# Projections as seven half products in a dense stage, both SSD scans run side by side with the plain rest of q and k

## The chip, the cores and the metric

The kernel runs on one core of a Trainium2 chip. Time is device microseconds of one execution. The engines are named as in the profile: PE is TensorE (matmul and transposes), PEld its weight load, DVE is VectorE, ACT is ScalarE, POOL is GpSimd, SP is SyncE, which issues all the DMAs here.

## The reference

One decoder layer over L = 1040 positions (16 meta tokens and 1024 real ones), width 1024, float32:

```python
h = rms_norm(x)                                   # (L, 1024)
z, xbc, dt, q, k, v = split(h @ W_in)             # 1024, 1024+2*256, 16, 1024, 1024, 1024 columns
# state-space half (SSD): 2 groups of 8 heads of 64, state 128, chunks of 128
xbc = silu(causal_dwconv4(xbc)); dt = softplus(dt + bias)
y[c] = (C B^T * decay) (x dt) + exp(cumsum) C prev;  prev = prev * chunk_decay + B^T (x dt decay)
y_ssd = rms_norm((y + D x) * silu(z))
# stick-breaking attention: 16 heads of 64
beta = sigmoid(q k^T / 8);  A[t,s] = beta[t,s] * prod_{s<j<t} (1 - beta[t,j]);  y_sb = A v
h += rms_norm([y_ssd ; rms_norm(y_sb)] @ W_out)
h += rms_norm((gelu(dwconv3(h W_g)) * (h W_u)) @ W_down)      # 2816 wide
```

## The kernel before

A float32 product is made of three fp32r matmuls: each operand is split into a high part (ACT casts it, `wh`, `whi`) and the rest (POOL subtracts it, `wl`, `wlo`), and hi·hi, hi·lo and lo·hi are added up in PSUM. Weights are split in tiles of 128x1024 by `load_w` (L155 on ACT, L156 on POOL).

The stages, in the order of the program:

- **Head.** x is loaded, normalised, transposed and split; the columns B0, C0 and dt are projected.
- **Projections.** `project_steps` (L169) makes one tile of 128 output columns at a time, over three ranges of tokens (400, 384 and 256 wide), with 24 matmuls for each: 8 blocks of 128 rows of W, three matmuls for each. The x, z, q, k and v columns are all made this way: `pj_X`, `pj_z`, `pj_q`, `pj_k`, `pj_v`. They are half steps of 12 matmuls, chained by `flow` and handed out by `run(fill, n)` between the small matmuls of the stages below, so that PE has work while the other engines prepare the next chunk or block.
- **Two scans**, one group after the other (155 to 402 us). For each of 9 chunks, `chunk_weights` makes the decay matrix (`sgh` on ACT, `sgl` on POOL at L627, matmul `sg`, `em` = exp on ACT, em times C·B at L641 on DVE) and two scaled copies of x (`xdt` at L644 on DVE, `yo` at L647 on POOL); `chunk_outputs` adds what the state gives (`yo` plus `yt` at L666 on DVE) and makes the next state (`xw` L670 and the sum L681 on DVE, `pv` L678 on POOL); `chunk_store` transposes, multiplies by silu(z) and sums the squares (L704 and L707 on POOL).
- **Attention** (404 to 897 us). For 8 pairs of heads p and 8 blocks of 128 queries i: `z` = q·k (L782); ACT takes both sigmoids, `kp` and `bt` (L783, L784); DVE runs a product scan over the keys, backwards, once for each head (`kp` and `hold`, L790); POOL multiplies `bt` by `kp`, once for each head (L792), and fills the edge `cb` (L793); PE transposes `bt` (`tw`, L804), ACT copies it (`th`), PE multiplies by v (`av`, L819). Block i has 144 + 128 i keys. z of a block stands three blocks ahead of its `tw` on PE; `kp` has two buffers, `bt` three. `split_q` splits q in each block on DVE (L758, L759). The fill between is q, k and v of the next pairs, and at the end the first steps of the output projection `mo`. v is transposed on PE (`vtp`).
- **Output projection, feed-forward, down projection**, to the end. The feed-forward and the down projection already use seven half products in place of eight (Strassen's scheme in Winograd's form: `fA`, `fX`, `fY`; `dnA`, `dnB`).

PE, DVE, ACT and POOL follow a written order in the feed-forward and the down projection; in the scans and the attention PE follows the order of the program and a scheduler orders the other engines.

## Time and profile before

| | |
|---|---|
| runs (us) | 1717.05, 1719.15, 1720.05; median 1719.15 |
| span of the profiled execution (us) | 1716.6, granted clock 0.999 |
| time of the profiled execution | not listed apart; the median is 2.55 us over its span |
| busy (us) | PE 1697.0, PEld 1495.9, DVE 1107.7, ACT 821.7, POOL 834.0 |
| scans 155 to 402 us, busy | PE 246.5, DVE 169.4, ACT 126.5, POOL 154.1 |
| attention 404 to 897 us, busy | PE 490.7, DVE 327.5, ACT 307.1, POOL 291.1 |
| DMA | 173.87 MB, 101 GB/s over the span |

A busy engine is one with an instruction in progress; an instruction that has started and is held up inside counts as busy. The duration of a matmul holds its fill and drain, so the pace of PE is read from one start to the next.

### The profile page before, as it was taken

The page shows a single profiled execution, that of the slowest core. Times are in us where ns is not written, and L with a number is a line of the kernel's source. Part 1 is how long each engine was busy: PE and PEld are TensorE (multiplying, and loading weights), DVE is VectorE, ACT ScalarE, POOL GpSimd, SP SyncE. Part 2 cuts the span into 40 slices and gives each one's busy share as a digit, 9 for nine tenths or more (in the row PEclk, how much of TensorE's full clock was granted, in tenths as well). Part 3 has the DMA queues.
Part 4 walks back from the last instruction along what each step waited for, and adds up shares of the span by engine and source line. Part 5 has one row for each costly group of instructions (what it writes and reads, how often), then busy time and mean ns, then how long its engine had stood idle before and what let it go on. Part 6 is the DMA issues. An engine that isn't in the chain of part 4 may idle for free.

```text
span 1716.6 us, 28052 instructions
## 1 busy us (share of the span) xinstructions
PE 1697.0 (99%) x11230; PEld 1495.9 (87%) x11230; DVE 1107.7 (65%) x1234; ACT 821.7 (48%) x1370; POOL 834.0 (49%) x641
## 2 busy tenths in 40 slices
PE   7999999999999999999999999999999999999998
PEld 6999889888989998998788788999988888888886
DVE  6752973875676686576640567676666566658777
ACT  5423563554665566567652445433333333344544
POOL 4323663686556575564552222587766777400001
PEclk9999999999999999999999999999999999999999
DMA  4132433231011011112223654233323323395335
GB/s 165 52 117 93 111 117 119 63 105 44 26 38 38 26 38 38 38 51 74 77 68 132 220 171 136 68 111 104 111 94 93 93 92 93 115 333 195 99 112 182
DMA packets 90674, 173.87 MB, mean 101 GB/s; under 512 B 10704, under 2 KB 35816, under 8 KB 90544
## 3 DMA queue, kind: packets, MB, share of 16 engines
q1 hardware_dynamic: 90544, 172.08, 31.8%
q8 instruction: 88, 1.44, 0.3%
q14 instruction: 42, 0.34, 0.1%
HBM read 122.32 MB, written 49.73 MB: 100 GB/s over the span
## 4 chain that ended last, share of the span: by engine, by line
PE 96%; DVE 1%; ACT 1%; DMA 1%; issue 0%; POOL 0%; SPq 0%; DVEq 0%; POOLq 0%; ACTq 0%
PE mo L976 10%; PE fX L1342 10%; PE dnA L1754 7%; PE fA L1342 7%; PE fY L1342 7%; PE pj_v L169 6%; PE pj_k L169 5%; PE pj_q L169 5%; PE pj_z L169 5%; PE dnB L1754 5%; PE pj_X L169 5%; PE av L819 4%; PE z L782 4%; PE tw L804 4%; PE pj_B L169 1%; PE yt L692 1%
## 5 line engine op out<-in xcount | busy, mean ns | idle before, releaser
L792 POOL TENSOR_TENSOR bt<-bt,kp 128x256 f32<-128x256 f32 (+7 forms) x128 | 212.1, 1677 | 184.2 <-DVE kp L790 140.6
L790 DVE TENSOR_TENSOR_SCAN kp<-kp,hold 128x272 f32<-128x272 f32 (+7 forms) x128 | 183.4, 1473 | 24.6 <-ACT kp L783 14.3
L1292 POOL TENSOR_TENSOR wlo<-wr,whi 128x1024 fp32r<-128x1024 f32 x43 | 99.3, 2318 | 40.5 <-ACT whi L1291 40.5
L1791 POOL TENSOR_TENSOR fms<-fms 128x1 f32<-128x1 f32 x8 | 2.5, 316 | 221.9 <-DMA ar<-fda 185.8
L783 ACT ACTIVATE kp<-z 128x288 f32<-128x288 f32 (+6 forms) x112 | 82.7, 739 | 50.7 <-PE z L782 25.8
L1291 ACT ACTIVATE whi<-wr 128x1024 fp32r<-128x1024 f32 x43 | 45.7, 1063 | 111.0 <-PE fX L1342 67.5
L169 PE MATMUL pj_v<-xs,wh_v 128*128 128x400 f32 (+2 forms) x384 | 95.0, 334 | 0.0
L169 PE MATMUL pj_k<-xs,wh_k 128*128 128x400 f32 (+2 forms) x384 | 94.6, 333 | 0.0
L1676 ACT ACTIVATE dh<-ar 128x512 fp32r<-128x512 f32 x77 | 48.6, 631 | 94.6 <-PE dnB L1754 44.7
L169 PE MATMUL pj_q<-xs,wh_q 128*128 128x386 f32 (+2 forms) x384 | 93.8, 331 | 0.0
L806 ACT ACTIVATE th<-tw 128x1024 f32<-128x1024 f32 (+2 forms) x96 | 75.5, 815 | 37.5 <-PE tw L804 37.2
L169 PE MATMUL pj_X<-xs,wh_X 128*128 128x400 f32 (+2 forms) x384 | 92.0, 326 | 0.0
L169 PE MATMUL pj_z<-xs,wh_z 128*128 128x386 f32 (+2 forms) x384 | 91.6, 326 | 0.0
L1414 DVE SCALAR_TENSOR_TENSOR ga<-gr,pp,ga 128x1024 f32<-128x1024 f32 x44 | 69.4, 1576 | 34.1 <-ACT ga L1407 33.4
L758 DVE CAST qh<-q 128x128 fp32r<-128x128 f32 x64 | 46.7, 731 | 68.9 <-PE z L782 68.5
L976 PE MATMUL mo<-woa,yh 128*128 128x512 f32 x256 | 85.5, 400 | 0.0
L1677 DVE TENSOR_TENSOR dl<-ar,dh 128x512 fp32r<-128x512 f32 x77 | 53.2, 691 | 47.2 <-ACT dh L1676 47.2
L784 ACT ACTIVATE bt<-z 128x288 f32<-128x288 f32 (+6 forms) x112 | 83.0, 741 | 0.0
L804 PE MATMUL tw<-ident,bt 128*128 128x128 f32 x576 | 75.7, 274 | 2.1 <-POOL cb L793 1.6
L819 PE MATMUL av<-th,v 128*64 128x128 f32 x1152 | 77.2, 278 | 0.0
L819 PEld LDWEIGHTS av<-th,v 128*64 128x64 f32 x1152 | 61.5, 136 | 13.8 <-issue 11.0
L804 PEld LDWEIGHTS tw<-ident,bt 128*128 128x128 f32 x576 | 65.4, 141 | 8.6 <-issue 3.1
(560 smaller groups left out, 5603.6 us busy)
## 6 DMA issues: line engine op xcount, KB each, us to landing
wr<-in_w_up SPq DMA_DIRECT2D x44, 512.0 KB
fds<-ga SPq DMA_DIRECT2D x44, 256.0 KB
b<-in_w_down SPq DMA_DIRECT2D x44, 256.0 KB
ar<-fds SPq DMA_DIRECT2D x44, 256.0 KB
fda<-ga SPq DMA_DIRECT2D x33, 256.0 KB
ar<-fda SPq DMA_DIRECT2D x33, 256.0 KB
yk<-yd SPq DMA_DIRECT2D x16, 512.0 KB
wor<-in_w_out SPq DMA_DIRECT2D x12, 512.0 KB
```

The costliest lines, as they stand in the source:

```text
L169: mm(acc[:ncol, :n - s], a[:, k, :ncol], xs[c0][:, b, k, s:n], start=(k == 0 and j == 0), stop=(k == KB - 1 and j == 2))
L783: nc.scalar.activation(kp[:, :, a:a + w], z[:, :, :w], AF.Sigmoid, scale=-QSCALE)
L784: nc.scalar.activation(bt[:, :, a:a + w], z[:, :, :w], AF.Sigmoid, scale=QSCALE)
L790: nc.vector.tensor_tensor_scan(kp[:, j][:, ::-1], kp[:, j][:, ::-1], hold[:, L - n:L][:, ::-1], 0.0, op0=ALU.mult, op1=ALU.max)
L792: nc.gpsimd.tensor_tensor(bt[:, j, 0:m], bt[:, j, 0:m], kp[:, j, 1:m + 1], op=ALU.mult)
L804: nc.tensor.transpose(tw[:, j, b, :], bt[:, j, c0:c0 + P], ident)
L806: copied[0] = nc.scalar.activation(th[:, :, :nb, :], tw[:, :, :nb, :], AF.Copy).ins
L819: mm(av[halves[j], :], v[:, kb, halves[j]], th[:, j, b, :], start=kb == 0, stop=kb == i)
L976: recent[0] = mm(acc, u[:, k, :], v[:, cs], start=(k == 0 and j == 0), stop=(k == 7 and j == 2))
L1292: nc.gpsimd.tensor_tensor(l, raw, h.bitcast(F32), op=ALU.subtract)
L1342: mm(acc[:, c, :nn], u[:, k, :], v[:, k, c0:c0 + nn], start=first and k == 0 and j == 0, stop=k == 3 and j == 2, skip_group_check=not first)
L1754: mm(banks[BANK[n], t], u[:, 0, c], v[:, 1, :], start=(n in (1, 2, 5) and p == 0 and i == 0), stop=(p == NPR - 1 and i == 2), skip_group_c ...
```

## The change

- **Dense stage.** x, z, the second B and C, and q and k of pairs 0 to 3 are made by 13 `Duo`s: two tiles of 128 columns each, over two halves of 520 tokens, as seven half products (`dA`, `dX`, `dY`) of 24 matmuls over 2 x 260 tokens in place of eight. The sums of token halves are made in the head (`t1` to `t4`), the sums of weights on POOL (`Duo.sums`), the sums of products on DVE. Convolution, silu and transposes of one duo are dealt out among the products of the next.
- **v** is made as tokens by channels, as seven half products of 128x512, so that the transposes of v go.
- Finished parts are stored in DRAM (`bcd`, `bnd`, `xsd`, `zd`, `qkd`, `vd`, `vcd`, `dtkd`) and loaded again where they are used. The first 16 rows of each block of v are copied from `vd` to `vcd`, DRAM to DRAM, ahead of the loads for the scans on SP's queue.
- **Both scans** run side by side, by chunk and then by group, 18 units. `xdt` and the sum `yo` + `yt` go from DVE to POOL; the squares are summed by one DVE reduction a chunk in place of additions on POOL.
- q and k of pairs 4 to 7 stay plain (`qk_fill`): 64 half steps of 12 matmuls over 260 columns, 4 ahead of the scans, 30 in them, 30 in the attention.
- **Attention**: q, k (already split) and v come from DRAM. The fill is 30 half steps of q and k, 9 short halo steps and 14 half steps of `mo`, spread evenly over the 64 blocks. The code of a block is otherwise the same (`L790` is L1106 now, L792 is L1108).

```diff
-CH = [(0, 400), (400, 384), (784, 256)]
+TH = L // 2
+CQ = TH // 2
+NQA = 4
+SCAN_FILL = 30
+OUT_FILL = 14
...
+    class Duo:
+        def sums(self):
+            r1, r2 = self.r
+            sub = nc.gpsimd.tensor_tensor
+            s24 = self.s24 = sa.tile([P, KB, P], F32, tag="s24", name=f"s24{self.nm}", bufs=1)
+            sub(r2[:, HI4], r2[:, HI4], r2[:, LO4], op=ALU.add)
+            sub(r2[:, LO4], r1[:, LO4], r2[:, LO4], op=ALU.subtract)
+            sub(s24[:, LO4], r2[:, HI4], r1[:, LO4], op=ALU.subtract)
+            sub(s24[:, HI4], r1[:, HI4], s24[:, LO4], op=ALU.subtract)
+        def product(self, n):
+            wn, xn, a, first = SPEC[n]
+            (hi, lo), (xh_, xl_) = self.w[wn], xo[xn]
...
+            for c in range(2):
+                for k in range(4):
+                    for j, (u, v) in enumerate(((hi, xh_), (hi, xl_), (lo, xh_))):
+                        mm(acc[:, c, :CQ], u[:, k, :], v[:, k, c * CQ:(c + 1) * CQ],
...
-            nc.vector.tensor_tensor(xdt[:nr], xsc, dt[:nr, c, hs].unsqueeze(2).to_broadcast([nr, 8, 64]),
+            nc.gpsimd.tensor_tensor(xdt[:nr], xsc, dt[:nr, c, hs].unsqueeze(2).to_broadcast([nr, 8, 64]),
...
-                nc.vector.tensor_tensor(yo[:nr], yo[:nr], yt[:nr], op=ALU.add)
+                nc.gpsimd.tensor_tensor(yo[:nr], yo[:nr], yt[:nr], op=ALU.add)
...
-            for b in range(0, 4, 2):
-                nc.gpsimd.tensor_tensor(sqk[:, b, ts], sqk[:, b, ts], sqk[:, b + 1, ts], op=ALU.add)
...
+            if g == 1:
+                nc.vector.tensor_reduce(out=sq[:, c0 + y0:c0 + nr],
+                                        in_=squares.pop(c)[:, :, ts].rearrange("p b t -> p t b"),
+                                        op=ALU.add, axis=mybir.AxisListType.X)
+        units = [(g, c) for c in range(NT + 1) for g in range(2)]
+        for n, (g, c) in enumerate(units):
+            nxt = chunk_weights(*units[n + 1]) if n + 1 < len(units) else None
+            scan_fill()
+            yo, zk, prev[g] = chunk_outputs(g, c, *cur, prev[g])
+            scan_fill()
+            chunk_store(g, c, cur[0], cur[1], yo, zk)
+            scan_fill()
+            cur = nxt
...
-    def split_q(p, i):
-        q = heads[p][0][:, NM + i * P:NM + (i + 1) * P]
...
-        nc.vector.tensor_copy(qh, q)
-        nc.vector.tensor_tensor(ql, q, qh.bitcast(F32), op=ALU.subtract)
...
+    for t in range(NT):
+        nc.sync.dma_start(out=vcd[NM * t:NM * t + NM], in_=vd[(t + 1) * P:(t + 1) * P + NM])
```

POOL in the scans, before: one chunk of one group in a steady stretch (`wl_z` belongs to the fill).

```order
L678 TENSOR_TENSOR pv_4_2277<-pv_3_2104,cdec 128x512
L647 TENSOR_TENSOR yo_5_2182<-xk_5_2153,dskip 128x512
L627 TENSOR_TENSOR sgl_6_2329<-tri,adl 128x1024
L704 TENSOR_TENSOR sqk_3_2148<-sqk_3_2148 128x128 x2
L707 TENSOR_TENSOR sq<-sqk_3_2148 128x128
L156 TENSOR_TENSOR wl_z_2570<-wr_z_2568,wh_z_2569 128x1024
```

POOL in the scans, now: the units of both groups in one chunk (`dtk` holds dt, its split parts and the decays).

```order
L940 TENSOR_TENSOR sgl_4_5148<-tri,dtk_4439 128x1024
L979 TENSOR_TENSOR yo_3_5007<-yo_3_5007,yt_3_5105 128x512
L991 TENSOR_TENSOR pv_4_5279<-pv_3_5112,dtk_4439 128x512
L957 TENSOR_TENSOR xdt_4_5172<-xk_4_5145,dtk_4439 128x512
L960 TENSOR_TENSOR yo_4_5174<-xk_4_5145,dskip 128x512
L940 TENSOR_TENSOR sgl_4_5240<-tri,dtk_4439 128x1024
L979 TENSOR_TENSOR yo_3_5099<-yo_3_5099,yt_3_5197 128x512
L991 TENSOR_TENSOR pv_4_5377<-pv_3_5204,dtk_4439 128x512
L957 TENSOR_TENSOR xdt_4_5264<-xk_4_5237,dtk_4439 128x512
L960 TENSOR_TENSOR yo_4_5266<-xk_4_5237,dskip 128x512
```

Two operations of 128x512 came to POOL for each unit, and the short additions of squares left it.

PE in the attention, before: from the transposes of block 4 of a pair to the products of block 5 with v, where z stands three blocks ahead.

```order
L804 MATMUL tw_4_0_4503<-ident,bt_4_4292 128x128 x8
L804 MATMUL tw_4_1_4514<-ident,bt_4_4292 128x128 x2
L169 MATMUL pj_q_400_4519<-xs_134,wh_q_4212 128x384 x2
L169 MATMUL pj_q_400_4519<-xs_134,wl_q_4213 128x384
L169 MATMUL pj_q_400_4519<-xs_134,wh_q_4212 128x384 x2
L169 MATMUL pj_q_400_4519<-xs_134,wl_q_4213 128x384
```

Now, at the same place of a pair:

```order
L1120 MATMUL tw_4_0_7479<-ident,bt_4_7314 128x128 x8
L1120 MATMUL tw_4_1_7490<-ident,bt_4_7314 128x128 x2
L1101 MATMUL z_7_0_7500<-qk_2_6685,qk_2_6681 128x348 x2
L1101 MATMUL z_7_0_7500<-qk_2_6685,qk_2_6683 128x348 x2
L1101 MATMUL z_7_0_7500<-qk_2_6687,qk_2_6681 128x348 x2
L1101 MATMUL z_7_1_7509<-qk_2_6685,qk_2_6681 128x348 x2
L1101 MATMUL z_7_1_7509<-qk_2_6685,qk_2_6683 128x348 x2
L1101 MATMUL z_7_1_7509<-qk_2_6687,qk_2_6681 128x348 x2
L1135 MATMUL av_4_7518<-th_4_0_7488,v_6847 64x128 x8
L1135 MATMUL av_4_7518<-th_4_1_7493,v_6847 64x128 x2
```

The fill behind the transposes is gone there; about one half step of 12 matmuls a block is left where two or more stood.

1028 lines of the change are left out of this document (636 added, 392 removed).

## Prediction, made before the changed kernel was run

> **What bounds the kernel now.** I read the page first, for the busy times and the chain that ended last:
>
> ```profile
> PE 1697.0 (99%) x11230; PEld 1495.9 (87%) x11230; DVE 1107.7 (65%) x1234; ACT 821.7 (48%) x1370; POOL 834.0 (49%) x641
> ...
> PE 96%; DVE 1%; ACT 1%; DMA 1%; issue 0%; POOL 0%; SPq 0%; DVEq 0%; POOLq 0%; ACTq 0%
> ```
>
> PE is idle for 1716.6 - 1697.0 = 19.6 us in all. So a matmul less is time won, as long as the others keep pace without it. The stretches by stage (columns: PE, PEld, DVE, ACT, POOL) tell how near they are, scans first, then attention:
>
> ```profile
> 155.00:402.00 247.00, 246.53 (x1620) 218.79 (x1621) 169.38 (x191) 126.47 (x274) 154.05 (x127) 1.00 0.35 100
> 404.00:897.00 493.00, 490.67 (x4068) 432.70 (x4067) 327.49 (x341) 307.13 (x513) 291.05 (x230) 1.00 0.15 45
> ```
>
> No engine but PE seems near its limit. But DVE and POOL hold each other up, which the sums hide. The timeline of both in the attention, DVE, then POOL:
>
> ```profile
> 616.56 3.51 DVE L790 TENSOR_TENSOR_SCAN kp<-kp,hold 128x784 f32<-128x784 f32 x2
> 620.44 1.06 DVE L758 CAST qh<-q 128x128 fp32r<-128x128 f32 x1 [0.37 <-PE z L782]
> 621.53 1.54 DVE L759 TENSOR_TENSOR ql<-q,qh 128x128 fp32r<-128x128 f32 x1
> 622.99 4.04 DVE L790 TENSOR_TENSOR_SCAN kp<-kp,hold 128x912 f32<-128x912 f32 x2
> ```
>
> ```profile
> 618.56 4.37 POOL L792 TENSOR_TENSOR bt<-bt,kp 128x768 f32<-128x768 f32 x2 [1.82 <-DVE kp L790]
> 622.87 0.30 POOL L793 TENSOR_TENSOR cb<-bt,kp 128x30 f32<-128x30 f32 x1
> ```
>
> ```profile
> L792 POOL TENSOR_TENSOR bt<-bt,kp x3: 412/1997/3840, 575.1 to 581.7; 128x1024 f32<-128x1024 f32 x2, 128x128 f32<-128x128 f32 x1
> ```
>
> Of two equal products of 128x1024, one lasted 3840 ns and the other 1997: the first began while the second scan was on DVE. At 618.56 the same: the second scan ended at 620.07, and the two products of 768 then took 2.86 us, 1.86 ns a column. And `ql` began at 621.53 and ended at 623.07, when POOL's products had ended (622.93). Each engine's instruction waits for the end of the other's. Where fill is thinnest, near 800 us, it goes on without a break:
>
> ```profile
> 801.69 3.47 DVE L790 TENSOR_TENSOR_SCAN kp<-kp,hold 128x784 f32<-128x784 f32 x2 [0.46 <-ACT kp L783]
> 806.62 2.47 DVE L905 SCALAR_TENSOR_TENSOR woa<-wor,pp,woa 128x1024 fp32r<-128x1024 f32 x1 [1.46 <-ACT woa L904]
> 809.02 1.26 DVE L962 TENSOR_TENSOR yl<-yk,yh 128x1024 fp32r<-128x1024 f32 x1
> ...
> 810.65 4.00 DVE L790 TENSOR_TENSOR_SCAN kp<-kp,hold 128x912 f32<-128x912 f32 x2
> 814.57 2.73 DVE L905 SCALAR_TENSOR_TENSOR woa<-wor,pp,woa 128x1024 fp32r<-128x1024 f32 x1
> ```
>
> ```profile
> 812.87 6.06 POOL L792 TENSOR_TENSOR bt<-bt,kp 128x896 f32<-128x896 f32 x2 [3.69 <-DVE kp L790]
> 818.89 1.22 POOL L793 TENSOR_TENSOR cb<-bt,kp 128x30 f32<-128x30 f32 x1
> ```
>
> From 810.65 to 818.93 scans, products and one split of `woa` stand end to end: 4.00 + 1.26 + 2 x 1.5 us. So for scans, products and their like the sum over both engines counts. In the attention before it was covered by 493 us of PE work. The change takes that cover away.
>
> **The change part by part.** Prices of PE, from the chain in order of time:
>
> ```profile
> 204.81 0.46 PE sg L634 x2
> 205.27 0.22 PE cb L638 x2
> 205.49 4.37 PE pj_X L169 x24
> 209.86 0.86 PE yf L662 x2
> 210.72 0.86 PE st L673 x2
> 211.58 4.17 PE pj_X L169 x24
> ```
>
> ```profile
> 389.31 2.87 PE pj_q L169 x24
> 392.18 0.44 PE vtp L428 x4
> 392.62 0.47 PE yt L692 x5
> ```
>
> ```profile
> 1110.44 2.88 PE fX L1342 x24
> ```
>
> ```profile
> 1503.86 26.75 PE dnA L1754 x118
> ```
>
> *Matmuls.* Counted in the order of the program, before: 28 groups of 24 at 4.37 (400 wide), 60 at 4.17 (384 or 386), 44 at 2.87 (256), and 72 transposes of v at 0.11: 122 + 250 + 126 + 8 = 506 us. Now: 127 groups of 24 over 260 columns at 2.88 (the feed-forward's 258 is the nearest row), 4 over 246 at 2.8, and 336 matmuls of 512 for v at 26.75 / 118 = 0.227, with 32 small ones: 366 + 11 + 76 + 3 = 456. dt loses 1. PE's work falls by **51 us**. If nothing else moved, the span would be 1716.6 - 51 = 1665.6.
>
> *Attention.* The columns of z over all blocks are 8 x 4736 = 37,888; PE's and POOL's own rows:
>
> ```profile
> 592.61 0.45 PE L782 MATMUL z<-kh,qh 64*128 64x400 f32 x2
> ...
> 593.36 1.97 PE L819 MATMUL av<-th,v 128*64 128x128 f32 x32
> ```
>
> ```profile
> 791.31 2.40 POOL L850 TENSOR_TENSOR sq<-sq,sqb 128x1024 f32<-128x1024 f32 x1
> ```
>
> z takes 0.75 us for 400 columns, 71 in all; 576 transposes at 0.11 take 63; 1152 `av` at 1.97 / 32 take 71. The fill is 30 x 12 matmuls at 0.12 = 43 and 14 x 12 at 0.227 = 38. PE: 286 us, where it was 491. DVE and POOL: the scans, 2 x 37,888 columns at 4.04 / 1824 = 2.2 ns, 168; the products, 73,728 columns at 1.9 ns (between 1.86 and 1.95), 140; 64 edges at 0.30, 19; six sums of squares at 2.40, 14; eight `woa` splits at 1.26 (`yl` has their size), 10. Together 351 us. The removed `split_q`, v's edges and the wl of v are already out of it. What is late next, then, is `tw`, which waits for `bt`; `z`, `av` and the fill stand behind it on PE. By blocks: block 7 needs 4.6 + 4.0 + 0.3 = 8.9 us of the pair, and PE has 1.95 + 1.76 + 1.97 + 1.3 = 7.0 for it; block 0 needs 1.4 against 2.3. The large blocks lose what the small can't give back. Term: 351 - 286 = **+65**. Bounds: 0, if the two engines were to run side by side (POOL alone has 173 and DVE 178), and +95, if each block also lost 0.5 us between hand-overs.
>
> *Scans.* Rows of the lines (ns: least, median, greatest):
>
> ```profile
> L627 POOL TENSOR_TENSOR sgl<-tri,adl x18: 393/1898/2893, 77.9 to 377.1; 128x1024 fp32r<-128x1024 f32 x16, 16x128 fp32r<-16x128 f32 x2
> L641 DVE TENSOR_TENSOR em<-em,cbm x18: 272/1638/2925, 157.5 to 385.1; 128x1024 f32<-128x1024 f32 x16, 16x128 f32<-16x128 f32 x2
> L644 DVE TENSOR_TENSOR xdt<-xk,dt x18: 674/764/2937, 127.4 to 382.4; 128x512 f32<-128x512 f32 x16, 16x512 f32<-16x512 f32 x2
> L647 POOL TENSOR_TENSOR yo<-xk,dskip x18: 1044/1204/1772, 127.5 to 384.1; 128x512 f32<-128x512 f32 x16, 16x512 f32<-16x512 f32 x2
> ```
>
> The gap between least and greatest is again the other engine. Undisturbed, a 128x512 takes 0.67 us on DVE and 1.04 on POOL, so moving `xdt` and `yo` + `yt` adds 2 x 0.37 to the sum of both, while the squares go from POOL. A unit now: `sgl` 1.90, four 128x512 on POOL 4.16, em times C·B 1.26, `xw` 0.67: 8.0 us; 16 units 128, the two short ones 6, four `wl` at 2.40 10: 144 us. PE: `sg` 0.92, `cb` 0.22, `yf` and `st` 1.72, 16 `yt` 1.5, so 4.4 a unit, 74 with the short ones, and fill 43: 117. The reduction of squares on DVE, eight times, reads one operand and lies beside PE's fill; I leave it at nothing, and 8 x 1.26 = 10 if it too must wait its turn. Term: **+27**; 0 if side by side, +45 if `sgl` and the rest stretch to their median as they did before.
>
> The Trainium skill (GPSIMD Engine Reference, section 4.1) calls POOL about twice as slow as DVE for operations with two inputs. By that the two moved would cost 1.34 each, and the scan term would be 10 us more; the rows say 1.55 times, and they stand.
>
> *Head, dense stage, boundaries.* Extra casts and differences in the head, waits of v's start for weights that are loaded into freed space, and the loads for the scans behind eight copies of `vcd` on SP show in no row. From below I take 5, from above the 19.6 us that PE idles now, twice. In the dense stage a pair of duos (x and z) asks POOL for about six splits of 128x1024 at 2.40 and eight sums of 128x512 at 1.04, and DVE for six taps and two scalings of 128x1040 at 1.26: 33 us beside 14 x 2.88 = 40 of PE, so it hides. Moves of `woa`, `qkd` stores and loads are hidden by 45 GB/s in the attention. Term: **+14**.
>
> *Sum:* 1716.6 - 51 + 65 + 27 + 14 = 1771.6, and the 2.55 us that the median lies over the span: **1774**. A difference under 0.2%, 3.4 us, could not be told from none.
>
> **Rivals.** *PE stays fed* (faster). Three blocks are under way at once, `bt` has three buffers, and a scan may wait less often than I sum up. Then the attention and the scans cost 10 together: 1716.6 - 51 + 10 + 14 + 2.5 = 1692. For it: before, PE lost only 493.0 - 490.7 = 2.3 us in the attention. Against: that stretch had 491 us of PE work. It decides where both terms fall below 35 together. The Trainium skill (SBUF — State Buffer, section "SBUF: two separate sides") bears on this: VectorE with two inputs from SBUF and GpSimd share a port pair, held for a whole instruction and never divided. The trace agrees wherever they meet (3840 against 1997 ns), but no row shows such a stage without PE's cover; by the rule the 351 us are a floor, and this rival falls.
>
> *The blocks' latency adds to it* (slower still). From the start of a block's scan (810.65) to the end of its products (818.93) pass 8.3 us, and PE stops at `tw` until then; `kp` has only two buffers, so ACT can't write the sigmoids of the block after next before the products of this one are done, and where ACT is late the two engines stand idle as well. Against: with 178 us of scans and splits beside 173 of products there is nearly always one waiting. At the upper bounds, 95 + 45 + 20: 1716.6 - 51 + 160 + 2.5 = 1828.
>
> *It comes out even.* Both terms at half (46) and a little at the boundaries: 1719.
>
> **How the numbers follow.** The sum as worked out, with terms between two thirds and the bounds: 0.68. PE stays fed: 0.15. Latency adds: 0.12. Even: 0.05. The likeliest gives 1774; its own range is 1735 to 1808. To hold 8 in 10 the range takes in the even case and part of the slow one: 1712 to 1812. Faster 0.15, same 0.05, slower 0.80.
>
> **What would show it.** Right: between the scans and the end of attention PE falls to about 80% busy, its idle time ends by `bt` or `cb` of POOL, and `bt` of 128x1024 often lasts over 3 us; the dense stage shows `dA`, `dX`, `dY` at 2.9 us for 24 without gaps; the scans take about 145 us, the attention about 350. Wrong: attention near 290 us with PE full, products at 2.0 us while scans run; or gaps of over 15 us at v's start or the scans' start.

## The result, and the profile after

The changed kernel takes 1831.2 us (median of 4 runs, 1828.8 to 1835.1), the one before 1719.6 (four runs now): ratio 1.066, 95% interval 1.064 to 1.068. The direction was forecast, the size was not: +112 us where the forecast had +54, outside its range of 1712 to 1812. The profiled execution has a span of 1831.3 us, 114.7 more than before.

First what the engines did. The page of the kernel after, busy time of each engine (part 1), and the granted clock in its 40 slices (part 2):

```profile
PE 1700.7 (93%) x11550; PEld 1465.1 (80%) x11550; DVE 1126.4 (62%) x1177; ACT 837.3 (46%) x1378; POOL 975.3 (53%) x687
...
PEclk9999999999799999998999999999999999999999
```

PE is busy 3.7 us longer than before, although it has less work, and idle for 1831.3 - 1700.7 = 130.6 us, where it was 19.6. Where, shows the busy time by stage: first before (head, scans, attention, rest), then after (head, dense stage, v, scans, attention, rest). The columns are the length, then busy us of PE, PEld, DVE, ACT and POOL, the granted clock, DMA share and GB/s.

```profile
0.00:154.50 154.50, 144.13 (x915) 137.31 (x915) 81.85 (x100) 60.04 (x106) 48.06 (x54) 1.00 0.34 110
154.50:401.00 246.50, 246.03 (x1619) 218.40 (x1618) 169.16 (x190) 126.42 (x273) 153.29 (x126) 1.00 0.35 100
401.00:917.70 516.70, 514.37 (x4255) 452.90 (x4253) 331.63 (x347) 315.70 (x524) 301.53 (x243) 1.00 0.15 45
917.70:1716.60 798.90, 792.49 (x4450) 687.26 (x4446) 525.02 (x597) 319.57 (x467) 331.08 (x220) 1.00 0.42 136
```
```profile
0.00:62.00 62.00, 42.87 (x305) 39.50 (x306) 47.16 (x60) 35.46 (x71) 26.16 (x41) 0.94 0.50 174
62.00:364.00 302.00, 287.07 (x2329) 283.47 (x2328) 152.46 (x146) 109.72 (x150) 184.77 (x107) 0.98 0.33 110
364.00:459.00 95.00, 89.53 (x455) 71.27 (x455) 41.60 (x40) 23.64 (x33) 19.96 (x8) 1.00 0.47 154
459.00:622.00 163.00, 136.85 (x893) 105.45 (x895) 108.68 (x126) 78.51 (x216) 122.25 (x87) 0.88 0.53 165
622.00:1031.00 409.00, 351.01 (x3122) 277.91 (x3122) 255.49 (x210) 269.44 (x442) 292.37 (x224) 0.96 0.28 89
1031.00:1831.30 800.30, 793.33 (x4456) 687.48 (x4452) 521.00 (x597) 320.55 (x467) 329.74 (x220) 1.00 0.42 136
```

Length less PE's busy time is PE's idle time: 58 us of the 131 are in the attention, 26 in the scans, 19 in the head, 15 in the dense stage. The clock column tells of a second loss: below 1.00, a busy microsecond does less work. Busy time times (1 - clock), summed over stretches of 4 us, is 2.7 us in the head, 5.8 in the dense stage, 17.1 in the scans and 14.6 in the attention: 40 us, an estimate from the rows, and about 1 before. What PE waits for, first in the attention, then in the scans, then in the head (us in total, times, longest):

```profile
PE z L1101 <- ACT th L1122: 35.3, 45, 4.3
PE tw L1120 <- ACT bt L1103: 12.6, 12, 4.3
PE z L1101 <- ACT bt L1103: 5.1, 8, 1.7
...
PE tw L1120 <- POOL bt L1108: 0.2, 1, 0.2
```
```profile
PE yt L1008 <- POOL yo L979: 21.2, 15, 2.9
PE sg L947 <- ACT sgh L938: 3.8, 1, 3.8
...
```
```profile
PE xtp L380 <- DVE xn L366: 14.9, 6, 8.4
...
```

In the attention, PE hardly ever waits for POOL. It waits for ACT: `z` and `tw` share two PSUM buffers, so `z` waits until ACT has copied `th` out of one, and `tw` until ACT has made the sigmoid `bt` from one. The scan and the product stretch as the prediction said (means 1.71 and 1.68 us), but PE's list has the product once, with 0.2 us, and the scan not at all:

```profile
L1106 DVE TENSOR_TENSOR_SCAN kp<-kp,hold 128x272 f32<-128x272 f32 (+7 forms) x128 | 212.6, 1706 | 106.1 <-ACT kp L1102 32.3
L1108 POOL TENSOR_TENSOR bt<-bt,kp 128x256 f32<-128x256 f32 (+7 forms) x128 | 212.5, 1679 | 103.8 <-DVE kp L1106 89.5
```

The clock, in stretches of 4 us at the start of the scans and in the middle of the attention (same columns):

```profile
472.00:476.00 4.00, 0.51 (x2) 0.30 (x2) 1.66 (x2) 2.49 (x9) 4.00 (x3) 1.00 0.10 33
476.00:480.00 4.00, 3.50 (x24) 2.43 (x24) 2.95 (x5) 1.30 (x3) 3.89 (x4) 0.52 0.33 79
480.00:484.00 4.00, 4.00 (x25) 2.88 (x25) 2.59 (x4) 0.48 (x1) 3.38 (x3) 0.50 0.75 154
484.00:488.00 4.00, 4.00 (x8) 1.58 (x7) 3.10 (x4) 3.15 (x11) 3.91 (x3) 0.50 0.32 37
488.00:492.00 4.00, 4.00 (x23) 2.76 (x22) 1.91 (x3) 0.00 (x0) 4.00 (x5) 0.50 0.64 198
...
848.00:852.00 4.00, 0.00 (x0) 0.00 (x0) 2.04 (x2) 2.22 (x4) 1.00 (x1) 0.95 0.71 218
852.00:856.00 4.00, 3.85 (x28) 3.39 (x30) 4.00 (x3) 3.16 (x6) 1.50 (x1) 0.50 1.03 421
856.00:860.00 4.00, 3.48 (x26) 2.91 (x24) 4.00 (x3) 1.52 (x3) 4.00 (x2) 0.70 0.61 244
```

After a stretch in which PE did next to nothing (0.51 and 0.00 of 4 us), it runs at half the clock, for 16 us and more the first time and some 6 the second; the matmuls show it too (one of `pj_k` over 260 columns lasts 0.42 us at 491.2 us and 0.28 at 497.4). The Trainium skill (TensorE: Matmul & The Clock Gate, section "HAM oscillation — how this bites in real kernels") gives the rule that PE should have no idle gaps over some 3.4 us; the trace agrees with it here, at 0.50 after gaps of 3.5 and 4.3 us. Shorter gaps were enough too: in the scans the clock was 0.57 from 510 to 514 and from 561 to 565 us, where the longest wait of PE just before was 2.3 us. The prediction did not count with any of it.

### The profile page after: what moved, and what is told of

Same layout as the page of the kernel before. It is cut to its first block, busy times and chain, and to the rows that moved or that the text cites. A ratio compares the mean times of both kernels' runs of the same rounds, so it can differ in the third digit from the quotient of the medians.

```text
span 1831.3 us, 29209 instructions
## 1 busy us (share of the span) xinstructions
PE 1700.7 (93%) x11550; PEld 1465.1 (80%) x11550; DVE 1126.4 (62%) x1177; ACT 837.3 (46%) x1378; POOL 975.3 (53%) x687
## 5 line engine op out<-in xcount | busy, mean ns | idle before, releaser
L1106 DVE TENSOR_TENSOR_SCAN kp<-kp,hold 128x272 f32<-128x272 f32 (+7 forms) x128 | 212.6, 1706 | 106.1 <-ACT kp L1102 32.3
L1108 POOL TENSOR_TENSOR bt<-bt,kp 128x256 f32<-128x256 f32 (+7 forms) x128 | 212.5, 1679 | 103.8 <-DVE kp L1106 89.5
L1101 PE MATMUL z<-qk,qk 64*128 64x328 f32 (+8 forms) x672 | 80.7, 356 | 41.3 <-ACT th L1122 35.3
L1101 PEld LDWEIGHTS z<-qk,qk 64*128 64x128 f32 x672 | 52.9, 192 | 64.4 <-ACT th L1122 49.4
L1120 PE MATMUL tw<-ident,bt 128*128 128x128 f32 x576 | 79.8, 281 | 15.5 <-ACT bt L1103 12.6
L1135 PE MATMUL av<-th,v 128*64 128x128 f32 x1152 | 83.0, 292 | 0.3 <-ACT th L1122 0.3
L1135 PEld LDWEIGHTS av<-th,v 128*64 128x64 f32 x1152 | 66.6, 145 | 14.5 <-issue 12.1
L1777 POOL TENSOR_TENSOR al<-wr,ah 128x512 fp32r<-128x512 f32 x20 | 28.7, 1433 | 76.9 <-ACT ah L1776 76.8
L2056 PE MATMUL dnA<-dl,dh 128*128 128x512 f32 x176 | 68.5, 389 | 0.0
L2056 PE MATMUL dnA<-dh 128*128 128x512 f32 x176 | 68.5, 389 | 0.0
L2056 PE MATMUL dnA<-dh,dl 128*128 128x512 f32 x176 | 68.5, 389 | 0.0
L2056 PE MATMUL dnB<-dh 128*128 128x512 f32 x132 | 51.3, 389 | 0.0
```

The lines of the kernel that those rows point to most:

```text
L1101: mm(z[:, j, :w], u[h, :], r[h, a:a + w], start=s_ == 0, stop=s_ == 2)
L1106: nc.vector.tensor_tensor_scan(kp[:, j][:, ::-1], kp[:, j][:, ::-1], hold[:, L - n:L][:, ::-1], 0.0, op0=ALU.mult, op1=ALU.max)
L1108: nc.gpsimd.tensor_tensor(bt[:, j, 0:m], bt[:, j, 0:m], kp[:, j, 1:m + 1], op=ALU.mult)
L1120: nc.tensor.transpose(tw[:, j, b, :], bt[:, j, c0:c0 + P], ident)
L1135: mm(av[halves[j], :], v[:, kb, halves[j]], th[:, j, b, :], start=kb == 0, stop=kb == i)
L2056: mm(banks[BANK[n], t], u[:, 0, c], v[:, 1, :], start=(n in (1, 2, 5) and p == 0 and i == 0), stop=(p == NPR - 1 and i == 2), skip_group_c ...
```

## The experiments

The prediction's reason is called the port theory below: VectorE and GpSimd, whose instructions were seen to wait for each other's end (3840 against 1997 ns in the prediction's row), set the length of both stages by the sum of their work. Its rival is the loop theory, in the attention also called the chain theory: one block or unit passes through TensorE, ScalarE, VectorE and GpSimd and back, in the order of each queue, and that chain sets the pace. Ratios are to the kernel before, measured along with each run; "against after" is the difference of the ratios times 1718 us. Stage times come from the profiled execution: length, idle time of PE and estimated slow clock, from the first `sg` to the first `z` (scans) and from there to the end of the last `av` (attention). Where its code was left as it is after, a profile showed the scans at 158 to 162 and the attention at 409 to 413, so a few us in a stage tell nothing.

| run | ratio, 95% interval | against after | scans: us, idle, slow | attention: us, idle, slow |
|---|---|---|---|---|
| after | 1.0659 (1.0639 to 1.0679) | | 162.3, 25.9, 17.1 | 409.8, 58.0, 14.6 |
| e1_bt_dve | 1.0566 (1.0547 to 1.0584) | -16 | | 395.7, 46.2, 14.8 |
| e2_scan_dve | 1.0629 (1.0606 to 1.0651) | -5 | 157.5, 22.0, 13.9 | |
| e3_dum_attn | 1.0906 (1.0889 to 1.0923) | +42 | | 455.7, 42.6, 9.3 |
| e4_dum_scan | 1.0680 (1.0663 to 1.0697) | +4 | 162.5, 10.1, 6.5 | |
| e6_fill_before_z | 1.0645 (1.0626 to 1.0665) | -2 | 158.3, 26.2, 13.0 | 408.5, 59.3, 15.1 |
| e8_scan_order | 1.0626 (1.0610 to 1.0642) | -6 | 151.6, 20.8, 10.9 | 411.0, 59.3, 16.1 |
| e9_all3 | 1.0424 (1.0402 to 1.0446) | -40 | 156.3, 20.0, 16.8 | 381.5, 36.8, 12.0 |
| e10_order_dve | 1.0642 (1.0626 to 1.0657) | -3 | 157.0, 26.1, 10.6 | |
| e13_dum_z | 1.0618 (1.0600 to 1.0635) | -7 | 160.5, 26.4, 15.5 | 406.5, 34.9, 6.7 |
| e14_zz3 | 1.0606 (1.0590 to 1.0621) | -9 | 158.4, 26.4, 13.0 | 403.3, 52.6, 16.0 |
| e15_bt4 | 1.0728 (1.0712 to 1.0744) | +12 | 157.7, 25.2, 12.8 | 433.0, 69.7, 17.4 |
| e22_deep_dve | 1.0627 (1.0612 to 1.0643) | -5 | 158.3, 26.3, 12.9 | 413.1, 53.4, 23.1 |
| e24_refill | 1.0642 (1.0621 to 1.0662) | -3 | 172.7, 17.8, 16.4 | 406.7, 63.2, 15.9 |
| e25_best | 1.0409 (1.0394 to 1.0425) | -43 | 157.9, 9.6, 9.5 | 380.6, 42.2, 13.9 |
| e26_sqb | 1.0658 (1.0642 to 1.0675) | 0 | 158.4, 26.3, 13.0 | 413.3, 56.2, 21.1 |
| e30_yo2x | 1.0745 (1.0726 to 1.0763) | +15 | 173.6, 34.6, 19.6 | |
| e31_scan_act | 1.0797 (1.0780 to 1.0814) | +24 | 184.4, 33.5, 20.7 | |
| e32_zz3_all | 1.0568 (1.0549 to 1.0587) | -16 | 151.9, 21.2, 10.9 | 403.6, 51.1, 21.3 |

**e1_bt_dve: the attention's products on VectorE.** The sum of both engines then has little of GpSimd left.

```diff
-            nc.gpsimd.tensor_tensor(bt[:, j, 0:m], bt[:, j, 0:m], kp[:, j, 1:m + 1], op=ALU.mult)
+            nc.vector.tensor_tensor(bt[:, j, 0:m], bt[:, j, 0:m], kp[:, j, 1:m + 1], op=ALU.mult)
...
-        nc.gpsimd.tensor_tensor(edges[p][:, :, i, 0:NM - 1], ...
+        nc.vector.tensor_tensor(edges[p][:, :, i, 0:NM - 1], ...
```

> The changed kernel with the products of bt and kp, and the edges, on DVE in place of POOL, in the attention only. Its attention lasts 414 us now (618 to 1032), of which PE idles 59.5 and loses about 14 to a lower granted clock. Port theory (DVE's scans and POOL's products exclude each other, 351 us in sum): DVE then has scans 168, products 73,728 columns at 1.04 ns 77, edges 10 and some 30 of other work, 285 us, less than PE's 326, so PE bounds again: attention about 345 us, kernel about 1763 us (-68), bt at about half of 1.9 ns a column with no instruction drawn out. Chain theory (a block's way through ACT, DVE, POOL and back to PE is too long for the three blocks in flight, whoever does the work): each block's way gets shorter by 0.9 us on average, a third of it counts: about -20 us, and PE still idles 45 us in the attention.

Measured -16, the stage 14 us shorter: what the chain theory said (-20), far from the port's -68. VectorE is busy 309.5 us there and GpSimd 38.0, held-up time included: 347 of 396 us, and PE still idles for 46. In this kernel the two engines' sum is not what holds the attention.

**e2_scan_dve: `xdt` and `yo` + `yt` back on VectorE**, where they were before the change.

```diff
-            nc.gpsimd.tensor_tensor(xdt[:nr], xsc, ...
+            nc.vector.tensor_tensor(xdt[:nr], xsc, ...
-                nc.gpsimd.tensor_tensor(yo[:nr], yo[:nr], yt[:nr], op=ALU.add)
+                nc.vector.tensor_tensor(yo[:nr], yo[:nr], yt[:nr], op=ALU.add)
```

> The changed kernel with xdt and the sum of yo and yt on DVE again, as before the change, in the scans only. The scans last 159 us now, PE idles 24.6 and loses about 17 to the clock. Port theory (sum of DVE's two-operand work and POOL's): 2 x 0.37 us less a unit, 12 us in 16 units: scans about 145 us, kernel about 1815 us (-16 with some of the clock). POOL theory (POOL alone is the bound, 7.2 us a unit): POOL loses 2.1 us a unit, PE bounds: scans about 122 us, kernel about 1793 us (-38). Neither (chain through the state): no change.

The scans take 157.5 us, within half a us of their spread, where the port theory had 145. The move of this work is not where the scans lost their time, and the sum of both engines alone does not set their length.

**e3_dum_attn and e4_dum_scan: TensorE work added**, whose results are overwritten: 18 matmuls of 128x128 ahead of `av` in each block, and 6 of 128x512 ahead of the `yt` products in each unit.

```diff
         av = psum_av(f"av{nm}")
+        for _ in range(18):
+            mm(av, identb, identb, start=True, stop=True)
```
```diff
             tp = psum_tp(f"yt{nm}")
+            for _ in range(6):
+                mm(tp.rearrange("p a b -> p (a b)"), xo["b22"][0][:, 0, 0:P], xo["b22"][0][:, 1, 0:512], start=True, stop=True)
```

> The changed kernel with 18 extra bf16 matmuls of 128x128 before each block's product with v, into the same PSUM tile, which the product then overwrites: about 1 us of PE work a block, 64 us in the attention, off the way from z to the transposes. Port theory: PE's own 326 plus 64 is 390, below the 414 that it lasts, so the kernel stays within 10 us of 1831, and PE's idle time falls by about 50. Clock theory (idle gaps of over 3 us bring half the clock for some us, 14 us lost in the attention): the granted clock there goes from 0.96 to about 1.00 and up to 14 us come back, so the kernel is equal or faster although it does more. If PE's work were the bound: +50 us or more.

> The changed kernel with 6 extra fp32r matmuls of 128x512 ahead of each unit's yt, into the PSUM tile that yt then overwrites: 1.4 us a unit, 24 us of PE work in the scans, at the place where PE waits for POOL's yo. Clock theory: the gaps before yt get too short to lower the clock, which goes from 0.88 to near 1.00 in the scans; 117 + 24 = 141 us of PE work fit in 159, so the scans get shorter by up to 17 us, kernel about 1817. If the clock costs nothing there (the engines that PE waits for set the pace): no change. If PE is the bound: +20 us.

In the attention 67 us of such work cost 42: at this place, between two hand-overs to ACT, work is on the path. In the scans 24 us of it cost some 4, inside the intervals, with the stage as long as before, and the idle time fell by 16 and the slow clock by 11: TensorE is not on the path of the scans at this place, and the half clock there fell into time that was waited anyway.

**e13_dum_z: the same kind of work where PE waits.** Nine of the small matmuls stand ahead of `z`.

```diff
+            av = None
+            if mix:
+                av = psum_av(f"avd{step}")
+                for _ in range(9):
+                    mm(av, identb, identb, start=True, stop=True)
             block = block_weights(p, i)
...
```

> In attention, 9 matmuls of 128x128 (bf16, overwritten later) per block just ahead of z, 62 blocks, about 32 us of TensorE work by what 18 of them cost ahead of av (67 us in 64 blocks, +43 us of time). Here they stand where TensorE waits for ScalarE's copy of tw, 35 us in 45 blocks. If the waits at this place are real slack: they cost 0 to 12 us (1831 to 1843), idle falls by 20 to 30, and the slow clock after gaps falls by 5 to 12 us. If work at this place delays the next hand-over to ScalarE by as much (TensorE's own part of the loop): +20 to +35.

The time does not rise; it falls by 7 us, with intervals that do not meet (1.0600 to 1.0635 against 1.0639 to 1.0679). The idle time fell by 23 us, the slow clock by 8. So in this place PE has slack, and filling it keeps the clock up. That it makes the kernel faster is less sure: of the 7 us the attention gave 3 (409.8 to 406.5), little outside the spread of 409 to 413.

**e6_fill_before_z: the plain products ahead of `z`.**

```diff
+            do(before)
             block = block_weights(p, i)
             next(block, None)
...
-            do(before)
             run(block)
```

> In attention, the plain output products of a block are issued ahead of its score products z instead of behind them, so that they stand between the transposes tw of an older block, whose PSUM buffers z takes over, and z. Nothing is added or left out. After spends 35.3 us of TensorE's idle time in attention in z waiting for ScalarE's copy th of tw, and 17.7 in z and tw behind the sigmoid bt. Theory 'no work between tw and z' (TensorE's order leaves nothing to do while ScalarE empties the shared buffers): most of the 35 goes and some comes back as waits of z's third chunk or of tw, -15 to -35 us against after (1796 to 1816), attention 375 to 395 instead of 410. Theory 'port' (VectorE and GpSimd together bound the stage): no change, within 5 us of 1831. Theory 'clock' (the slow stretches after gaps are a cost of their own): the slow-clock loss in attention, 14.6 us, falls along with the idle time.

The idle time only changed its name. PE's waits in this run from 622 to 1031 us (its attention is 614 to 1023):

```profile
PE z L1101 <- ACT th L1122: 19.1, 14, 4.3
PE tw L1120 <- ACT bt L1103: 11.1, 20, 1.4
PE tw L1120 <- POOL bt L1108: 9.5, 7, 2.8
```

Now `tw` waits for POOL's product, which the fill between `z` and `tw` had covered. The same fill can't stand in both places: that is the cover which the change has spent.

**e14_zz3, e15_bt4, e26_sqb: one resource of the attention more.** Three z/tw buffers, for which mo gets one accumulator and `av` shares a bank; four blocks under way; a buffer of its own for the squares.

```diff
-        return stage[0][1].tile([P, 2, 512], F32, tag="zz", name=name, bufs=2)
+        return stage[0][1].tile([P, 2, 512], F32, tag="zz", name=name, bufs=3)
...
```
```diff
-        btt = ap.tile([P, 2, L], F32, tag="bt", name=f"bt{nm}", bufs=3)
+        btt = ap.tile([P, 2, NM + (i % 4 + 5) * P], F32, tag=f"bt{i % 4}", name=f"bt{nm}", bufs=1)
-            if len(turn) > 2:
+            if len(turn) > 3:
```
```diff
-            sqt = ap.tile([P, 2, 4, P], F32, tag="th", name=f"sqb{p}", bufs=2)...
+            sqt = ap.tile([P, 2, 4, P], F32, tag="sqb", name=f"sqb{p}", bufs=1)...
```

> In attention, three double-bank PSUM buffers for z and tw instead of two; to make room, the plain products mo get one accumulator instead of two, and av shares one bank with the small turns (the sums of squares for r_ssd are taken in one go). Same work. After: attention 410 us, TensorE idle 58, of it 40 in z and 13 in tw, all behind ScalarE's copies and sigmoids of these buffers; with the fill moved ahead of z the idle time stayed (59) and only changed its name. Theory 'two buffers' (TensorE and ScalarE hand two buffers to and fro, and that hand-over sets the pace): a third lets TensorE run ahead, idle time falls by 25 to 45 us with some of the 14.6 us of slow clock: 1780 to 1805. Theory 'block latency' (TensorE waits for what ScalarE, VectorE and GpSimd need for one block, sigmoid, scan and product, and ScalarE is late because kp has two buffers): waits move from z to tw, within 8 us of 1831. Theory 'port': the same, no change.

> In attention, four blocks under way instead of three (four bt buffers, and tw of a block is issued one block later). Same work. Theory 'block latency': tw's waits for bt (13 us) go and, as ScalarE is no longer held up, part of z's: -15 to -40 us against 1831. Theory 'two buffers' (the hand-over of the z and tw buffers between TensorE and ScalarE sets the pace): within 8 us of 1831. Theory 'port' (VectorE and GpSimd bound the stage): within 5 us too.

> In attention, the squares of a head's outputs (sqb, 128x1024, once a head) get a buffer of their own instead of one of the two of th. Same work. After, ScalarE waits 12.0 us in the stage (3 times) with the copy th at the head of its queue, until GpSimd has added sqb into the sums, and everything behind it on ScalarE waits too. Theory 'head of ScalarE's queue' (TensorE's waits for th are in large part ScalarE waiting for GpSimd): -5 to -12 us. Theory 'port': no change (within 3 us). Theory 'closed loop with other waits ready to take over' (as the third buffer, the fourth block and the moved fill showed, -8, +13 and -2): within 4 us.

None of them is the cause alone: -9, +12 and 0 us. In e14_zz3 `z` waits 2.7 us for `th` instead of 35.3, but 14.1 for `bt`, and `avc` 10.3 in the bank that it now shares. In e15_bt4, which issues `tw` a block later, PE is idle for 69.7 us, and no theory had it slower. In its trace `tw` waits 8.7 us for POOL's `bt` (0.2 in after) and once 5.9 us for a load of `qk`, and `avc` 4.8 for DVE (0.9); whether these cost the 23 us is not shown.

**e22_deep_dve: all three of e1_bt_dve, e14_zz3 and e15_bt4**, the edges one block later. (Diffs as above.)

> All that loosens the attention together: three z/tw buffers, four blocks under way (the edges one block later), and bt*kp with its edges on VectorE. If the attention is bound by TensorE's own work once these are loosened: 340 to 360 us instead of 410, idle below 20, slow clock below 8: 1765 to 1785. If idle stays above 35 (as with bt*kp on VectorE and the fill moved, 37), a further limit is there (ScalarE's queue, 268 us busy, or VectorE with 311): 1795 or more. Before's 1718 is out of reach in every case, since TensorE's busy time in the stage is 337 us at the full clock and the scans are untouched.

Not 340 to 360 us but 413, with 53 us idle: the branch with a further limit, and it is slower than e1_bt_dve alone. The list of waits names new places (`av` for `th` 13.2, `z` for `bt` 10.2, `pj_k` for the emptying of its accumulator 7.0).

**e8_scan_order, e10_order_dve: the scans' order.** A unit's outputs are issued ahead of the next unit's weights; in the second, with the edit of e2_scan_dve as well. The reason is in the timeline of after, one unit (start, us, engine, in brackets the idle time before; PE's fill and weight loads left out):

```profile
537.65 0.39 PE L947 MATMUL sg<-sgh,lowr 128*128 128x512 f32 x1
537.85 1.09 ACT L949 ACTIVATE em<-sg 128x512 f32<-128x512 f32 x2 [0.46 <-PE sg L947]
...
538.33 1.02 PE L975 MATMUL yf<-pv,ct 128*128 128x512 f32 x2
...
539.71 1.99 DVE L954 TENSOR_TENSOR em<-em,cbm 128x1024 f32<-128x1024 f32 x1
...
540.58 2.88 POOL L940 TENSOR_TENSOR sgl<-tri,dtk 128x1024 fp32r<-128x1024 f32 x1
...
541.63 0.68 DVE L977 TENSOR_TENSOR yt<-yf,dtk 128x512 f32<-128x512 f32 x1
...
543.43 1.71 POOL L979 TENSOR_TENSOR yo<-yo,yt 128x512 f32<-128x512 f32 x1
...
545.18 0.66 PE L1008 MATMUL yt<-ident,yo 128*128 128x128 f32 x4 [2.57 <-POOL yo L979]
```

`yf` of this unit is ready at 539.35, 2.3 us before DVE uses it, but DVE first multiplies the next unit's `em`, and its `sg` stands ahead of `yf` on PE. `yt` is done at 542.31, and then POOL, at an `sgl` until 543.46, is not free for the sum.

```diff
-            nxt = chunk_weights(*units[n + 1]) if n + 1 < len(units) else None
             scan_fill()
             yo, zk, prev[g] = chunk_outputs(g, c, *cur, prev[g])
+            nxt = chunk_weights(*units[n + 1]) if n + 1 < len(units) else None
```

> In the scans, the outputs part of a unit (yf, yt, yo, xw, st) is issued ahead of the weights part of the next unit (sg, em, cb) instead of behind it. So VectorE no longer multiplies the next unit's em before it makes this unit's yt, for which GpSimd's yo and TensorE's yt turn wait. Nothing is added or left out. Theory 'loop' (one unit's chain through TensorE, ScalarE, VectorE, GpSimd and back to TensorE sets the pace, about 9.9 us a unit): the wait of the turn for yo, 19.6 us in all, mostly goes; the scans go from 162 to 130-148 us and some of the 17 us of slow clock goes with it: 1797 to 1817. Theory 'port' (sum of VectorE and GpSimd, 144 us by the prediction): scans stay at or above 144 us less what they wait for today, so 1813 or more. A loop that only turns round (now em is late, and the turn's first products wait for it): within 6 us of 1831.

> The scans' new order (outputs ahead of the next weights) and xdt and yo's sum on VectorE instead of GpSimd. Alone the move to VectorE gave -4 us. Theory 'loop': the chain from yf to the turn now is VectorE's yt and its sum on one engine, without a crossing to GpSimd, and it is shorter than in the new order alone: scans 125 to 140 us, 1 to 8 us less than the new order alone. Theory 'GpSimd is the pace of the scans in the new order': a further 10 to 20 us. If VectorE is the pace then (133 us busy with the moved work), scans no less than about 140 and this is no better than the new order alone or up to 10 us worse.

The scans fall to 151.6 us, 6 to 11 less than in the unchanged order, not to the 130 to 148 that the loop theory gave; PE still waits 15.2 us for `yo`. Two runs below that have this order show 151.9 and 156.3. With the work on VectorE as well it is 157.0, where the loop theory had 125 to 140. So the order is at most a part, and what holds the stage then is not shown.

**e30_yo2x, e31_scan_act: more for the pair, and less.** In the first, `yo`'s first product is made twice; in the second, it and `xdt` go to ScalarE.

```diff
             nc.gpsimd.tensor_tensor(yo[:nr], xsc, dskip[:nr, hs]...)
+            nc.gpsimd.tensor_tensor(yo[:nr], xsc, dskip[:nr, hs]...)
```
```diff
-            nc.gpsimd.tensor_tensor(xdt[:nr], xsc, dt[:nr, c, hs]...)
+            for h8 in range(8):
+                nc.scalar.activation(xdt[:nr, h8], xsc[:, h8], AF.Copy, scale=dt[:nr, c, 8 * g + h8:8 * g + h8 + 1])
...
-            nc.gpsimd.tensor_tensor(yo[:nr], xsc, dskip[:nr, hs]...)
+            for h8 in range(8):
+                nc.scalar.activation(yo[:nr, h8], xsc[:, h8], AF.Copy, scale=dskip[:nr, 8 * g + h8:8 * g + h8 + 1])
```

> In the scans, GpSimd makes the first product of yo (x times D, 128x512, 1.04 us undisturbed) twice per unit, with the same result: 18 products more, 17 to 19 us of the pair VectorE and GpSimd. Theory 'port sum' (the prediction's term: 144 us, the sum of what both do on SBUF, sets the scans): scans 162 + 17 = 179, the whole 1848. Theory 'loop' (one unit's chain TensorE, ScalarE, VectorE, GpSimd, TensorE sets the pace, and this product is not on it but stands on GpSimd ahead of links that are): 0 to +8, 1831 to 1839. The scans' new order gained 8 us and the move of two products to VectorE 4, so neither alone has explained the stage so far.

> In the scans, GpSimd's two first products of a unit (xdt and x times D for yo, 128x512 each) are made by ScalarE, as 8 activations of 128x64 with a scale each. So 2.08 us a unit, about 35 us in all, leave GpSimd's queue and the pair's sum, and nothing of them comes to VectorE; ScalarE, 78 us busy in the scans, gets 288 small activations. Theory 'GpSimd and VectorE as a pair' (doubling one such product cost 13.5 us of 17): the scans fall by 20 to 35 us, to 125-140: 1797 to 1812. Theory 'loop' (doubling cost so much only because that product stands right ahead of yo's sum in GpSimd's queue): -5 to -15 us, 1816 to 1826. If ScalarE, with 16 more instructions a unit between em and the next sgh, becomes the pace: 1831 to 1850.

The first looks like the port theory: 15 of 17 us, where the loop theory had 0 to 8. The second fits neither: with some 35 us taken from the pair, the scans grow by 22. The busy times of the scans in this second run:

```profile
456.00:641.00 185.00, 151.26 (x889) 108.23 (x889) 101.64 (x126) 146.04 (x505) 75.57 (x51) 0.88 0.46 140
```

No engine is full there (PE 151 at a clock of 0.88, DVE 102, ACT 146, POOL 76 of 185). PE's wait has moved: 19.4 us for DVE's `em`, which stands behind ACT, and 3.4 for `yo`, where it was 21.2. So this is near the branch in which ScalarE becomes the pace (1831 to 1850 expected, 1855 measured), and it does not tell what paced the scans without this edit. Work added to POOL and work added to ACT both lengthen the scans, work added to PE ahead of the `yt` products does not: that points to a chain through ACT, DVE and POOL, but the loop theory's numbers came true in none of its runs (e8, e10, e30, e31).

**e9_all3, e24_refill, e25_best, e32_zz3_all: together.** e9_all3 joins e1_bt_dve, e6_fill_before_z and e8_scan_order; e24_refill moves cover:

```diff
-SCAN_FILL = 30
-OUT_FILL = 14
+SCAN_FILL = 44
+OUT_FILL = 18
```

e25_best is both of these; e32_zz3_all is e9_all3 with the third buffer of e14_zz3.

> Three edits together: the plain products ahead of z, the scans' outputs ahead of the next weights, and the attention's products bt*kp with their edges on VectorE instead of GpSimd (alone: -15 us). If the parts add up: -15 -25 -25, about 1766 us (1745 to 1790). If all the idle time that they touch is one and the same chain, less than the sum: 1790 to 1810. By the port theory the attention would gain some 50 us over after. It is below before (1718) only if TensorE's own work in the two stages has no excess over the prediction's prices (286 and 117 us), which the profile of after does not support (its busy time in attention is 352 us).

> The cover is placed where TensorE was idle: 44 steps of the plain projections lie in the scans instead of 30 (14 x 1.44 = 20 us of TensorE work out of attention, where e4 found room for 24 us), and 18 quarters of the output product lie in attention instead of 14 (4 x 2.7 = 11 us out of the rest). Same work in all. Theory 'other engines pace both stages': scans unchanged (162), attention 410 less at most a few, the rest 11 shorter: -8 to -15, 1816 to 1823. Theory 'TensorE's own work paces attention': scans +15 to +20, attention -10, rest -11: within 6 us of 1831. If attention's pace is work and the scans' is not: scans unchanged, attention -10, rest -11, with some slow clock: -20 to -30.

> What helped, together: bt*kp with the edges on VectorE, the fill ahead of z, the scans' outputs ahead of the next weights (these three: 1793 us), and the cover placed anew (44 steps in the scans, 18 quarters in attention). If the refilling adds to it as it does alone: 1775 to 1785. If the scans, already at TensorE 131 busy of 152 us, take the 20 us as time: 1790 to 1800. It remains above before (1718) in either case.

> The three edits that came to 1793 us (products bt*kp on VectorE, fill ahead of z, the scans' outputs first), and the third z/tw buffer added (one accumulator mo instead of two, av and the small turns in one bank). In the first three alone attention is 381.5 us with 36.8 idle and 12.0 of slow clock; with the refilling TensorE waited 22.6 us in tw for the sigmoid bt and 11.7 in z for ScalarE. Theory 'the hand-over of two buffers is what is left': idle falls by 15 to 25, 1763 to 1778. Theory 'ScalarE's queue as a whole is late, whichever buffer': within 8 us of 1793.

e9_all3 gains more than its parts: -40 where they give -16, -2 and -6 alone. Its attention is 28 us shorter, twice what e1_bt_dve gave, so the fill ahead of `z`, worth nothing while POOL was late, is worth 14 us once POOL is out of the way. What PE still waits for in its attention:

```profile
PE tw L1120 <- ACT bt L1103: 23.2, 45, 3.4
PE z L1101 <- ACT th L1122: 5.8, 10, 2.1
PE z L1101 <- ACT bt L1103: 4.2, 7, 2.3
```

e24_refill took 9 us of PE work out of the attention, net, and its time fell by 3 while the idle time rose by 5: PE's own work alone does not set this stage. Its scans rose by 10 to 14 with 20 us more work, so e4_dum_scan's free room was free for work at one place only. In e25_best the scans with the same 20 us more take 157.9 us, against 151.6 and 156.3 for the new order without it, and the rest of the program is 12 us shorter. 1787 us is the best of these runs, still 4.1% above before. The third buffer made e9_all3 25 us slower: `z` waits for ACT almost no longer, and in its place stand `av` behind `th` and two waits at the places where banks were merged (`avc`) or an accumulator was taken away (`pj_k`):

```profile
PE av L1140 <- ACT th L1127: 11.2, 9, 2.7
PE avc L1160 <- ACT ysc L1143: 10.8, 7, 2.6
PE pj_k L220 <- DVE st L870: 9.2, 5, 3.4
```

So whether two buffers for `z` and `tw` are the last limit stays open: no run could add one without taking another away.

## Why the prediction was wrong

The four terms of the sum, against the two profiled executions (idle time gained, and slow clock, by stage):

| term | predicted | measured |
|---|---|---|
| matmuls | -51 | -37: PE's busy time, in after less the 40 us of slow clock, 1697.0 to 1660.5 |
| attention | +65 | +70: idle 58.0 - 2.3, slow clock 14.6 |
| scans | +27 | +42: idle 25.9 - 0.5, slow clock 17.1 |
| head, dense stage, boundaries | +14 | +38: idle 46.7 - 16.8, slow clock 8.5 |
| sum | +55 | +114 (the spans differ by 114.7) |

- **The slow clock is missing from the sum.** Idle time alone rose by 111 us, against 106 predicted over the three terms (56, 25 and 30, against 65, 27 and 14). That sum came out near; that PE then works at half rate after its gaps, an estimated 40 us, was in no term. The 40 us are what the rows hold, not what a full clock would save: where it was halved (e4_dum_scan) the scans stayed as long, and where 8 us of it went in the attention (e13_dum_z) the time fell by 7 with 23 us less idle.
- **Matmuls, mis-sized by 14 us, and in the attention by 50.** The prediction priced the attention's matmuls at 286 us; PE's busy time there, at full clock, is 351 - 14.6 = 336. One part can be counted: the stage holds 216 matmuls of mo (each of eight pairs of operands 18 times, each of eight more 9 times) where the prediction had 14 x 12 = 168, at 0.227 us 11 more. This is not part of the 14 us of the total, since the stage held 216 of them before as well, and both kernels make 768. Counted from each matmul's start to the next start or to its own end, with the slow clock taken off (an estimate from the records), the projections fell by 61 us, 536 to 475, more than predicted, while the same 576 transposes `tw` took 74 us instead of 60 and the same 672 of `z` 72 instead of 67. These two stand at PE's new waits, where nothing follows to cover a matmul's end; that this is the reason is a reading of the records that no run tested.
- **Attention: the term held by luck, the mechanism did not.** The step that failed is "for scans, products and their like the sum over both engines counts", as the bound of the stage. The stage is 410 us, not 351; the term came out near only because the matmuls, which are taken off, were also short by 50. With the products off POOL the stage fell by 14, where the port theory gave 68. PE waits for ACT, not for `bt` and `cb` of POOL. The stretches are there (POOL's products 212.5 us where 140 was counted), but are mostly waited for by nobody on PE. The sum was also not the one that its own stretch gives: 1.5 us for a product of 896 columns is 1.7 ns a column, where the sum takes 1.9, some 17 us more. POOL's part, as far as the waits tell, is indirect: ACT waits at the head of its queue for `kp`'s buffer, and everything behind it waits too:

```profile
ACT kp L1102 <- POOL cb L1109: 17.7, 12, 3.4
ACT th L1122 <- POOL sq L1166: 12.0, 3, 4.7
```

Taking the second of these away gained nothing (e26_sqb).

- **Scans: the port sum was too low a bound.** 144 was predicted, 162 measured (158 to 162 over the runs). One price in it was short: the sum `yo` + `yt` takes 1.27 us on POOL undisturbed, not 1.04, and 0.68 on DVE in e2_scan_dve, so 1.9 times and not 1.55; that is 4 us. That the sum of VectorE and GpSimd alone does not set the pace is shown by e2_scan_dve, which made it at least 12 us smaller and gained nothing to speak of, and by e8_scan_order, which left it as it was and gained 6 to 11. What does set it stays open: a unit's chain through ACT, DVE and POOL fits the direction of e4, e8 and e30, but its forecasts missed, and e30 fits the sum better. PE's price for the stage, 117 us, held: 119.8 at full clock.
- **Head, dense stage and boundaries: mis-sized by 24 us.** In the head PE waits 14.9 us for DVE's `xn`; in the dense stage it is idle for 14.9 us by the rows above. At v's start, where the prediction feared waits, little came: PE idles 5.5 us in the 95 of that stage. No experiment was made on these.
- **The rivals.** "PE stays fed" fell. The prediction had let it fall by the Trainium skill's rule (SBUF — State Buffer, section "SBUF: two separate sides") that VectorE and GpSimd hold a shared port pair one at a time; the runs do not show it by that rule, since e1_bt_dve left POOL 38 us of work and PE was still idle for 46 us. "The blocks' latency adds to it" gave 1828, three from the result, by adding up upper bounds, and its waits of ACT for `kp` are in the trace; but its place was `tw` behind POOL's products, 0.2 us here, so the number is luck too, and one block more under way, which should have cured it, cost 12 us.
- **What is shown and what is not.** Shown: 84 of PE's 131 us of idle time, and an estimated 32 of its 40 us of slow clock, lie in the two stages that lost their cover; that the sum of VectorE and GpSimd alone sets neither stage (e1, e2, e8); that work on PE is free at two places where it waits (e13, e4); that POOL's products are worth 16 us in the attention alone, and with the fill ahead of `z` 28 us of the stage. Not settled: which hand-over sets the remaining 37 us of e9_all3's attention, and what paces the scans, in the old order and in the new.

## What to carry to other kernels

Matmul time that is saved where PE was full is only worth what the same matmuls did not cover elsewhere: here 37 us were saved and 151 us of waiting and slow clock came up. Price a stage that has lost its cover as a chain of hand-overs in the order of the queues, PE's waits for PSUM copies on ACT among them, not only as the busy time of its fullest pair of engines, and look at what PE has to do between two hand-overs. Where short gaps will open on PE, add the granted clock to the sum; work that is issued inside the gaps cost next to nothing here at two places (e4, e13), and 42 of its 67 us at a third (e3).

## What the hardware did that was not expected

- The clock stayed at 0.50 for longer than the gap before it: 0.51 of 4 us busy, then 16 us at 0.50 to 0.52, twelve of them with PE busy throughout. The Trainium skill (TensorE: Matmul & The Clock Gate, section "What's actually happening") has the full rate return after at least one busy window, of some 3.4 us; here those twelve us, over three such windows, did not bring it back, and the measurement decides.
- The clock also fell where PE had waited for no more than 2.3 us at a time (0.57 from 510 to 514 us).
- Thirty-two us (an estimate from what 18 a block cost in e3_dum_attn) of useless matmuls did not make the kernel slower (e13_dum_z, -7 us), with the clock of the attention at 0.98 instead of 0.96.
